# Streaming encoder step: head loads moved from the POOL queue to the SP queue as 64-row pieces, head 0 loaded during the last projection group, one store for both parts of q or k

## The chip, the cores and the metric

The kernel runs on one core of one Trainium2 chip. The metric is device time in microseconds, the median of several executions. TensorE (PE) does the matmuls, VectorE (DVE), ScalarE (ACT) and GpSimd (POOL) the elementwise work; transfers are issued from SyncE's queue (SP) and from POOL's queue.

## What is computed

One layer of a chunk-causal encoder, in float32, over 2048 prompt frames and 8 x 16 sample frames. The part around the change is the mixer:

```python
proj = h @ w_in
q, k, v, u_val, u_gate = jnp.split(proj, [D_ATT, 2 * D_ATT, 3 * D_ATT, 3 * D_ATT + D_CONV], axis=-1)
...
s = jnp.einsum("bqhd,bkhd->bhqk", qc, kc) * scale + bias      # 9-chunk band, 8 heads of 64
p = jax.nn.softmax(s, axis=-1)
att = jnp.einsum("bhqk,bkhd->bqhd", p, vc)
...
u = u_val * jax.nn.sigmoid(u_gate)
c = silu(layernorm(depthwise_conv(u, width 31)))
y = jnp.concatenate([att, c], axis=-1) @ w_out
```

Cross-attention into 256 memory tokens and a SwiGLU feed-forward layer of 2816 hidden channels follow, each with norms and a residual.

## The kernel before, in words

Float32 products are made from two float32r parts, a high part (the rounded value) and a low part (the rest), in three matmuls (`mm3`, L281 to L283). Tokens are tiles of 128: 16 prompt tiles and one sample tile.

`phase_proj` goes through the tiles in three groups of two sub-groups: tiles 0 to 5, 6 to 11, and 12 to 15 with the sample tile. Each group makes the GLU projections (4 blocks), v (L657 stores it), and q and k in four blocks j of 128 channels, two heads each. `qk` evicts one block: ACT writes the high part, DVE the low part, into tiles `qh` and `ql` of two buffers each (in the last group `qhx`, `qlx`), and two stores (L713, L714) put them into the DRAM buffers `qs[j]` and `ks[j]`, laid out [part, channel, token]. The convolution taps run as background generators: `conv_vector` on DVE (L522), `conv_pool` on ACT and POOL (L531, L532), then `conv_norm` (L537 to L557), which transposes on PE, normalizes, goes through tanh and stores.

Normalized inputs of a sub-group lie in the pairs `hh0`/`hl0` to `hh2`/`hl2` in turn, 12 KB a partition each, in the arena `sbR`. The arenas are laid out by hand: a tag is a ring of buffers at an offset in KB, and a later stage's tile on the same bytes waits until the earlier readers are done.

`attention` goes through 8 heads of 16 tiles: `scores` (L845, two matmuls per key range: q's two parts stacked on 128 rows as `q2`, against k's high part on both halves of the rows, `k2`, and the same for the low part, `kl`), `softmax_band` (L760 on DVE with the head's bias tile `bt`, L762 on ACT), `transp` (L862 to L864) four units later, `values` (L875) two units after that, once for four tiles. One sample's attention (`sample`) is interleaved with each head. `load_head` loads a head: q2, k2, kl and v2 on POOL's queue, 1 MB each, and `bt` on SP's queue (L829). Buffers exist for an even and an odd head, so that head h + 2 reuses those of head h. In program order the load of the next head stands at tile 6 of a head.

```python
nc.gpsimd.dma_start(q2[:, :], self.qs[jj][:, rr, :])
for c, dst in ((0, k2), (1, kl)):
    nc.gpsimd.dma_start(dst[:, :], self.ks[jj][c, rr, :].unsqueeze(0).to_broadcast([2, DH, NPT * P]))
nc.gpsimd.dma_start(v2[:, :, :], self.vs[h // 4][:, h % 4, :, :])
```

The order of the instructions on each engine and queue is set by a scheduler that plays the program through with its own costs: it takes what is ready by then, the earlier in the program first (the conv background with a lowered priority). Each engine and queue then runs in that order and waits where it must. `mixout` follows with the output projection; its weights are loaded and split by `out_weights` during the last head.

Of the kernel before, what the change touches and what calls it, by code (L numbers as in the profile page):

```python
# [8 lines left out]
F32 = mybir.dt.float32  # L9
F32R = mybir.dt.float32r  # L10
# [7 lines left out]
P = 128  # L18
D = 1024
KC = D // P  # L20
NPT = 16
S_TILE = 16
H = 8
DH = 64
# [9 lines left out]
NEG = -1e30  # L34
# [102 lines left out]
class Build:  # L137
# [22 lines left out]
    def early(self, ctx):  # L160
        phases = self.phases
        inner = ctx.enter_context(ExitStack())
        fa, fb = self.fa, self.fb = self.flex(ctx, (8192, F32)), self.flex(inner, (4096, F32))
        sbF, sbR, ps = self.sbF, self.sbR, self.ps
        self.w = Region().lay(sbF, 0, ("wf", 4, 3)).lay(sbR, 72, ("wh", 4, 4), ("wl", 4, 4))
        self.psa = Region().lay(ps, 0, ("mm", 2, 4), ("tr", 4, 2))
        self.ap = (Region()
                   .lay(sbF, 12, ("gbc", 4, 1), ("xt", 4, 2), ("junk", 2, 1), ("ut", 3.1171875, 6))
                   .lay(sbF, 12, ("qhx", 1.5, 2), ("qlx", 1.5, 2), ("kxx", 0.5, 2), ("vo", 1, 3), ("ko", 2, 5))
                .lay(sbF, 44.75, ("us", 5.75, 1), ("cwt", 0.484375, 1), ("cvec", 0.0625, 1), ("half", 0.0625, 1))  # L170
                   .lay(fb, 0, ("ct", 3, 5), ("bst", 0.03125, 2), ("bmv", 0.03125, 2), ("ss", 0.03125, 6),
                        ("rstd", 0.03125, 6))
                   .lay(fa, 0, ("xn", 2, 2), ("z", 2, 2), ("th", 2, 1), ("sg", 1.5, 2), 
                        ("ctmp", 3, 2), ("qh", 1.5, 2), ("ql", 1.5, 2), ("kx", 0.5, 2))
                   .lay(sbR, 0, *[(f"h{c}{i}", 12, 1) for i in range(3) for c in "hl"])
                   .lay(sbR, 104, ("vv", 2, 2)))
        smp = Region().lay(fa, 28, ("qsamp", 2, 1), ("ksamp", 2, 1))
        self.qsamp = self.t(smp, [P, 4, P], F32, "qsamp")
        self.ksamp = self.t(smp, [P, 4, P], F32, "ksamp")
        if "mem" in phases:  # L180
            self.phase_mem()
        if "proj" in phases:
            self.phase_proj()
        if "att" not in phases:
            return
        self.kept = Region().lay(sbF, 0, ("attT", 32, 1), ("sums", 0.5, 1), ("attS", 2, 1))
        self.attT = self.t(self.kept, [P, 4, NPT * P], F32, "attT")
        self.sums = self.t(self.kept, [P, NPT, H], F32, "sums")
        self.attS = self.t(self.kept, [P, 4, P], F32, "attS")
        self.attention()  # L190
        inner.close()
        with ExitStack() as c:
            self.mixout(c)
# [251 lines left out]
    def phase_proj(self):  # L445
        nc, A = self.nc, self.A
        pool = self.ap
        ps_mm = ps_tr = Region().lay(self.ps, 0, ("mm", 2, 4), ("tr", 2, 2), ("ca", 4, 1))
        self.lo_engine = nc.gpsimd
        big = [P, KC, 3 * P]  # L450
# [23 lines left out]
        def norm_sub(sub):  # L474
            hh = self.t(pool, big, F32R, f"hh{self.nsub % 3}", 1)
            hl = self.t(pool, big, F32R, f"hl{self.nsub % 3}", 1)
# [99 lines left out]
        for gi, subs in enumerate(GROUPS):  # L576
# [4 lines left out]
            t0 = tiles[0]  # L581
            hs = nxt
            uts = []
# [93 lines left out]
            def qk(which, j, blk, x):  # L677
# [5 lines left out]
                sh = self.t(pool, [P, 3 * P], F32R, "qh" + x_, 2)  # L683
                sl = self.t(pool, [P, 3 * P], F32R, "ql" + x_, 2)
# [56 lines left out]

    def attention(self):
        nc, A = self.nc, self.A
        sbF, sbR, ps, fa, fb = self.sbF, self.sbR, self.ps, self.fa, self.fb
        pool = (Region().lay(sbF, 34.5, ("kc", 4, 2), ("kt", 4.25, 1), ("pp", 1.5, 1), ("vn", 2, 1))
                .at("z", 2.5, (fa, [15, 17.5, 20, 22.5, 25]), (fb, [0, 2.5, 5]))
                .lay(fb, 7.5, ("vc", 4, 2), ("nmx", 0.03125, 12), ("sm", 0.03125, 2))
                .lay(fa, 0, ("qbd", 2.5, 2), ("otmp", 2, 1), ("bs", 1.0625, 1)).lay(fa, 10, ("bt", 2.5, 2))
                .at("q20", 8, (sbR, [0])).at("k20", 8, (sbR, [8])).at("kl0", 8, (sbR, [16])).at("v20", 8, (sbR, [72]))
                .at("q21", 8, (sbR, [24])).at("k21", 8, (sbR, [32])).at("kl1", 8, (sbR, [40])).at("v21", 8, (sbR, [80]))  # L750
                .lay(sbR, 48, ("ph0", 10, 1), ("pl0", 10, 1)).lay(sbR, 88, ("ph1", 10, 1), ("pl1", 10, 1)))
# [3 lines left out]
        row = [P, NPT * P]  # L755
# [61 lines left out]
        def load_head(h):  # L817
            jj, odd = h // 2, h % 2
            rr = slice(odd * DH, (odd + 1) * DH)
            q2 = self.t(pool, row, F32R, f"q2{odd}", 1)  # L820
            k2 = self.t(pool, row, F32R, f"k2{odd}", 1)
            kl = self.t(pool, row, F32R, f"kl{odd}", 1)
            v2 = self.t(pool, [P, NPT, P], F32R, f"v2{odd}", 1)
            nc.gpsimd.dma_start(q2[:, :], self.qs[jj][:, rr, :])
            for c, dst in ((0, k2), (1, kl)):
                nc.gpsimd.dma_start(dst[:, :], self.ks[jj][c, rr, :].unsqueeze(0).to_broadcast([2, DH, NPT * P]))
            nc.gpsimd.dma_start(v2[:, :, :], self.vs[h // 4][:, h % 4, :, :])
            bt = self.t(pool, [P, W5], F32, "bt", 2)
            nc.sync.dma_start(bt[:, :], toep[h][:, :])  # L829
            nc.gpsimd.memset(bt[:DH, W5 - DH:], NEG)  # L830
            nc.gpsimd.memset(bt[DH:, :DH], NEG)
            return q2, k2, kl, v2, bt

# [51 lines left out]
        heads = {0: load_head(0)}  # L885
# [14 lines left out]
        for i in range(n + LV + 1):  # L900
            if i < n:
# [3 lines left out]
                if t == 6 and h + 1 < H:  # L905
                    heads[h + 1] = load_head(h + 1)
# [19 lines left out]
    def selectors(self):  # L926
# [3 lines left out]
            self.sbR, 68, ("expand", 2, 1), ("rt", 0.5, 3), ("rs", 0.0625, 2))  # L930
# [22 lines left out]
    def out_weights(self):  # L953
# [3 lines left out]
        for k, (o, engine) in enumerate(zip((0, 8, 16, 72, 24, 32, 48, 56), "PPPPVPVP")):  # L957
# [9 lines left out]
    def mixout(self, ctx):  # L967
# [10 lines left out]
                .at("kvh", 4, (sbR, [64, 80]), (fr, [8])).at("kvl", 4, (sbR, [104, 84]), (fr, [12])))  # L978
# [706 lines left out]
```

## Time and profile before

| | |
|---|---|
| median of 3 runs | 3066.88 us (3065.92 to 3074.45) |
| span of the profiled execution | 3068.5 us (the page gives no other time of it) |
| PE, DVE, ACT, POOL busy | 96%, 70%, 44%, 46% |
| granted TensorE clock, mean | 0.980 |
| moved by SP's queue, by POOL's queue | 427.53 MB, 69.70 MB |

How to read it: times in a row are microseconds from the start of the span. A row of the timeline is start, duration, engine, line, operation, output <- input, and in brackets how long the engine had stood before it and what ended that. Tiles show as the arena they lie in (sbr, sbx, sbf, flexb, psb for PSUM), DRAM buffers by name. Busy shares are averages over stages; what a stage could give is read from the waits inside it. "Granted clock" is the share of full speed that the throttle gave TensorE.

### The profile page before, as it was taken

How to read it: one execution, taken by the hardware profiler on the slowest of the kernel's cores; microseconds unless marked ns; L12 is line 12 of the kernel's file. 1: busy time of each engine (PE TensorE's matmuls, PEld its weight loads, DVE VectorE, ACT ScalarE, POOL GpSimd, SP SyncE). 2: the span in 40 equal slices, each digit the busy share in tenths (PEclk: the TensorE clock that was granted, in tenths of full speed). 3: DMA queues.
4: the chain of work that ended last, by engine and by line, in shares of the span. 5: the costliest groups of instructions: out<-in, count | busy, mean ns of one | idle time of the engine just before them, and what ended most of it. 6: DMA issues, size and time to landing. Idle time of an engine off the chain costs nothing.

```text
span 3068.5 us, 46049 instructions
## 1 busy us (share of the span) xinstructions
PE 2958.1 (96%) x16924; PEld 2725.9 (89%) x16924; DVE 2135.7 (70%) x3077; ACT 1358.3 (44%) x2718; POOL 1419.9 (46%) x1336
## 2 busy tenths in 40 slices
PE   8999999968999999999999999999999999999998
PEld 8999999957888788788888999999999999888786
DVE  6696886746668456635456888877878999556565
ACT  4544455546767344423234333443334444433432
POOL 0267595621112324325355655555555776524413
PEclk9999999978999999999999999999999999999999
DMA  8635252645663456423246333454425345756664
GB/s 302 246 111 176 90 172 97 189 150 135 155 158 141 147 205 209 168 69 124 91 157 206 132 135 135 149 176 159 154 105 174 144 144 178 261 186 210 217 202 161
DMA packets 217693, 500.17 MB, mean 163 GB/s; under 512 B 40757, under 2 KB 104765, under 8 KB 208627
## 3 DMA queue, kind: packets, MB, share of 16 engines
q1 hardware_dynamic: 181035, 427.53, 41.6%
q0 software_dynamic: 36432, 69.70, 7.3%
q8 instruction: 133, 2.18, 0.3%
q14 instruction: 93, 0.76, 0.1%
HBM read 365.97 MB, written 141.81 MB: 165 GB/s over the span
## 4 chain that ended last, share of the span: by engine, by line
PE 38%; DMA 4%; DVE 3%; issue 2%; POOL 2%; ACT 1%; SPq 0%; DVEq 0%; POOLq 0%; ACTq 0%
PE psb L283 12%; PE psb L282 12%; PE psb L281 12%; DMA sbf<-in_w_down_dram 2%; PE psb L289 1%; POOL sbf L1536 1%; DMA sbf<-x 1%; PE psb L1391 1%; DMA sbf<-hn 0%; DVE sbr L1597 0%; DVE sbr L1540 0%; DVE sbr L1414 0%; POOL sbf L338 0%; DMA sbf<-in_w_gate_dram 0%; DVE flexb L1476 0%
## 5 line engine op out<-in xcount | busy, mean ns | idle before, releaser
L281 PE MATMUL psb<-sbr 128*128 128x384 f32 (+3 forms) x2808 | 945.6, 338 | 11.1 <-DVE sbf L688 7.1
L282 PE MATMUL psb<-sbr 128*128 128x384 f32 (+3 forms) x2356 | 808.5, 343 | 2.6 <-DVE sbr L318 2.4
L283 PE MATMUL psb<-sbr 128*128 128x512 f32 (+3 forms) x1848 | 633.4, 344 | 2.7 <-DVE sbr L1597 2.5
L281 PEld LDWEIGHTS psb<-sbr 128*128 128x128 f32 x2808 | 533.0, 190 | 41.0 <-DVE sbf L688 7.3
L283 PE MATMUL psb<-sbr,sbx 128*128 128x384 f32 (+2 forms) x1484 | 478.5, 323 | 0.0
L282 PEld LDWEIGHTS psb<-sbr 128*128 128x128 f32 x2356 | 448.1, 190 | 29.3 <-DVE sbr L318 2.7
L283 PEld LDWEIGHTS psb<-sbr 128*128 128x128 f32 x1848 | 348.6, 189 | 31.6 <-DVE sbr L1597 4.9
L289 PE MATMUL psb<-sbr 128*128 128x512 f32 x1200 | 295.5, 394 | 3.0 <-DVE flexb L1044 1.7
L1414 DVE TENSOR_TENSOR sbr<-sbf,sbr 128x512 fp32r<-128x512 f32 x258 | 263.5, 1024 | 40.7 <-ACT sbr L1413 40.0
L1413 ACT CAST sbr<-sbf 128x512 fp32r<-128x512 f32 x258 | 159.3, 620 | 280.5 <-PE psb L282 232.3
L283 PEld LDWEIGHTS psb<-sbr,sbx 128*128 128x128 f32 x1484 | 282.7, 191 | 0.1
L522 DVE SCALAR_TENSOR_TENSOR psb<-sbf,psb 128x768 f32<-128x768 f32 (+1 forms) x290 | 264.5, 912 | 6.2
L289 PEld LDWEIGHTS psb<-sbr 128*128 128x128 f32 x1200 | 222.4, 189 | 48.7 <-DVE flexb L1044 2.1
L1597 DVE TENSOR_TENSOR sbr<-sbf,sbr 128x384 fp32r<-128x384 f32 (+1 forms) x231 | 168.4, 752 | 93.7 <-ACT sbr L1596 91.2
L276 POOL TENSOR_TENSOR sbx<-sbf,sbr 128x1024 fp32r<-128x1024 f32 x60 | 150.9, 2517 | 85.8 <-ACT sbr L275 81.2
L1596 ACT CAST sbr<-sbf 128x384 fp32r<-128x384 f32 (+1 forms) x231 | 110.7, 497 | 167.7 <-PE psb L282 150.1
L1536 POOL TENSOR_TENSOR sbf<-sbf 128x512 f32<-128x512 f32 x77 | 105.7, 1377 | 168.3 <-DMA sbf<-in_w_down_dram 166.7
L532 POOL TENSOR_TENSOR flexb<-flexb,flexb 128x128 f32<-128x128 f32 (+1 forms) x180 | 168.5, 936 | 30.9 <-ACT flexb L531 20.3
L281 PE MATMUL psb<-sbr,sbx 128*128 128x384 f32 (+1 forms) x524 | 170.6, 327 | 1.2 <-ACT sbr L1393 0.7
L1413 ACT CAST sbx<-sbf 128x512 fp32r<-128x512 f32 x153 | 94.7, 621 | 161.6 <-PE psb L282 152.7
L1414 DVE TENSOR_TENSOR sbx<-sbf,sbx 128x512 fp32r<-128x512 f32 x153 | 151.5, 992 | 15.7 <-ACT sbx L1413 15.5
L1408 POOL TENSOR_TENSOR sbf<-sbf 128x512 f32<-128x512 f32 x66 | 98.6, 1493 | 107.6 <-DVE sbr L1414 50.8
(339 smaller groups left out, 6294.0 us busy)
## 6 DMA issues: line engine op xcount, KB each, us to landing
af<-flexb SPq DMA_DIRECT2D x33, 1344.0 KB, 5.6
sbf<-in_w_down_dram SPq DMA_DIRECT2D x154, 256.0 KB, 3.9
sbf<-af SPq DMA_DIRECT2D x90, 384.0 KB, 4.0
sbf<-in_w_gate_dram SPq DMA_DIRECT2D x66, 512.0 KB, 3.3
sbf<-in_w_up_dram SPq DMA_DIRECT2D x66, 512.0 KB, 3.5
sbf<-x SPq DMA_DIRECT2D x49, 512.0 KB, 3.9
sbf<-in_w_in_dram SPq DMA_DIRECT2D x48, 512.0 KB, 4.2
sbr<-ks POOLq DMA_DIRECT2D x16, 1024.0 KB, 33.9
```

The costliest lines, as they stand in the source:

```text
L276: self.lo_engine.tensor_tensor(lo[:, :], wf[:, :], hi[:, :].bitcast(F32), ALU.subtract)
L281: nc.tensor.matmul(ps, lh, rh, start=start, stop=False, **kw)
L282: nc.tensor.matmul(ps, lh, rl, start=False, stop=False, **kw)
L283: nc.tensor.matmul(ps, ll, rh, start=False, stop=stop, **kw)
L289: nc.tensor.matmul(y[o], l, r[:, o * 512:(o + 1) * 512], start=start and x == 0, stop=stop and x == 2)
L522: nc.vector.scalar_tensor_tensor(acc if w < CW - 1 else o, src(w), cwt[:, j, w:w + 1], acc, ALU.mult, ALU.add)
L532: nc.gpsimd.tensor_tensor(o, o, v, ALU.add)
L1413: nc.scalar.copy(hs[j][:, :], src[j])
L1414: nc.vector.tensor_tensor(ls[j][:, :], src[j], hs[j][:, :].bitcast(F32), ALU.subtract)
L1536: nc.gpsimd.tensor_tensor(acc[:, :], acc[:, :], q[:, :], ALU.add if s > 0 else ALU.subtract)
L1596: nc.scalar.copy(ch[:, m], a[:, x, m])
L1597: nc.vector.tensor_tensor(cl[:, m], a[:, x, m], ch[:, m].bitcast(F32), ALU.subtract)
```

## The change

- A head is loaded from SP's queue, in seven transfers: k2, q2 and kl each as two pieces of 64 rows (lower half, upper half), and v2. The pieces can cover a range of tiles.
- Head 0 is loaded in two steps: tiles 0 to 11 at the start of the last projection group, tiles 12 to 15 after block j = 0 of q and k in that group. Heads 1 to 7 are loaded whole, at the same place of the program as before.
- Buffers move so that head 0's are free in the last group: the last sub-group (one prompt tile and the sample tile) gets its own smaller pair `hhz`/`hlz` at 56 to 72 KB of `sbR`; `v20`, `ph`/`pl` (the transposed probabilities) and `v21` lie elsewhere; the softmax tiles `z`, the bias tiles `bt`, two of the split output weights and a few small tiles too.
- `qh` and `ql` become one tile `qk` of two parts, and one store writes both.

```diff
-                   .lay(sbF, 12, ("qhx", 1.5, 2), ("qlx", 1.5, 2), ("kxx", 0.5, 2), ("vo", 1, 3), ("ko", 2, 5))
+                   .lay(sbF, 12, ("qkx", 3, 2), ("kxx", 0.5, 2), ("vo", 1, 3), ("ko", 2, 5))
...
+                   .lay(sbR, 56, ("hhz", 8, 1), ("hlz", 8, 1))
...
             hs = nxt
+            if last:
+                first = self.head_tiles(0)
+                self.head_load(0, first, 0, t0)
...
-                nc.sync.dma_start(dst[0, :, col:col + npc], sh[:, :npc].bitcast(F32))
-                nc.sync.dma_start(dst[1, :, col:col + npc], sl[:, :npc].bitcast(F32))
+                nc.sync.dma_start(dst[:, :, col:col + npc].rearrange("c p n -> p c n"),
+                                  sp[:, :, :npc].bitcast(F32))
...
+                if last and j == 0:
+                    self.head_load(0, first, t0, NPT)
+                    self.head0 = first
...
+    def att_pools(self):
+        sbF, sbR, fa, fb = self.sbF, self.sbR, self.fa, self.fb
+        self.attp = (Region().lay(sbF, 34.5, ("kc", 4, 2), ("kt", 4.25, 1), ("pp", 1.5, 1), ("vn", 2, 1))
+                     .at("z", 2.5, (fa, [24]), (fb, [0, 2.5, 5]), (fa, [9, 11.5, 14, 16.5]))
+                     .lay(fb, 7.5, ("vc", 4, 2), ("nmx", 0.03125, 12), ("sm", 0.03125, 2))
+                     .lay(fa, 0, ("qbd", 2.5, 2), ("otmp", 2, 1), ("bs", 1.0625, 1)).lay(fa, 19, ("bt", 2.5, 2))
+                     .lay(sbR, 0, ("q20", 8, 1), ("k20", 8, 1), ("kl0", 8, 1), ("q21", 8, 1), ("k21", 8, 1), ("kl1", 8, 1),
+                          ("v20", 8, 1), ("ph1", 10, 1), ("pl1", 10, 1), ("v21", 8, 1))
+                     .lay(sbR, 88, ("ph0", 10, 1), ("pl0", 10, 1)))
+
+    def head_tiles(self, h):
+        nc, pool, odd = self.nc, self.attp, h % 2
+        row = [P, NPT * P]
+        q2, k2, kl = [self.t(pool, row, F32R, f"{n}{odd}", 1) for n in ("q2", "k2", "kl")]
+        v2 = self.t(pool, [P, NPT, P], F32R, f"v2{odd}", 1)
+        bt = self.t(pool, [P, 5 * P], F32, "bt", 2)
+        nc.sync.dma_start(bt[:, :], self.toep[h][:, :])
+        nc.gpsimd.memset(bt[:DH, 5 * P - DH:], NEG)
+        nc.gpsimd.memset(bt[DH:, :DH], NEG)
+        return q2, k2, kl, v2, bt
+
+    def head_load(self, h, tiles, a, b):
+        nc = self.nc
+        q2, k2, kl, v2, _ = tiles
+        c = slice(a * P, b * P)
+        rr = slice(h % 2 * DH, (h % 2 + 1) * DH)
+        for o in range(2):
+            half = slice(o * DH, (o + 1) * DH)
+            for dst, src in ((k2, self.ks[h // 2][0]), (q2, self.qs[h // 2][o]), (kl, self.ks[h // 2][1])):
+                nc.sync.dma_start(dst[half, c].bitcast(F32), src[rr, c])
+        nc.sync.dma_start(v2[:, a:b, :].bitcast(F32), self.vs[h // 4][:, h % 4, a:b, :])
...
-                .at("z", 2.5, (fa, [15, 17.5, 20, 22.5, 25]), (fb, [0, 2.5, 5]))
...
-        heads = {0: load_head(0)}
+        heads = {0: self.head0}
...
-                    heads[h + 1] = load_head(h + 1)
+                    heads[h + 1] = self.head_tiles(h + 1)
+                    self.head_load(h + 1, heads[h + 1], 0, NPT)
...
-        for k, (o, engine) in enumerate(zip((0, 8, 16, 72, 24, 32, 48, 56), "PPPPVPVP")):
+        for k, (o, engine) in enumerate(zip((0, 8, 16, 48, 24, 32, 72, 56), "PPPPVPVP")):
```

More of the change, by code (lines that the diff above doesn't have):

```diff
@@ L173, in early @@
                    .lay(fa, 0, ("xn", 2, 2), ("z", 2, 2), ("th", 2, 1), ("sg", 1.5, 2),
-                        ("ctmp", 3, 2), ("qh", 1.5, 2), ("ql", 1.5, 2), ("kx", 0.5, 2))
+                        ("ctmp", 3, 2), ("qk", 3, 2), ("kx", 0.5, 2))
                    .lay(sbR, 0, *[(f"h{c}{i}", 12, 1) for i in range(3) for c in "hl"])
+                   .lay(sbR, 56, ("hhz", 8, 1), ("hlz", 8, 1))
                    .lay(sbR, 104, ("vv", 2, 2)))
@@ L179, in early @@
         self.ksamp = self.t(smp, [P, 4, P], F32, "ksamp")
+        self.att_pools()
         if "mem" in phases:
@@ L449, in phase_proj @@
         self.lo_engine = nc.gpsimd
-        big = [P, KC, 3 * P]
         gbc = self.gain(pool, "g_mix_pre", "gbc")
@@ L474, in norm_sub @@
         def norm_sub(sub):
-            hh = self.t(pool, big, F32R, f"hh{self.nsub % 3}", 1)
-            hl = self.t(pool, big, F32R, f"hl{self.nsub % 3}", 1)
+            x = self.nsub % 3 if len(sub) == 3 else "z"
+            hh, hl = [self.t(pool, [P, KC, len(sub) * P], F32R, f"h{c}{x}", 1) for c in "hl"]
             self.nsub += 1
@@ L682, in qk @@
                 tick()
-                sh = self.t(pool, [P, 3 * P], F32R, "qh" + x_, 2)
-                sl = self.t(pool, [P, 3 * P], F32R, "ql" + x_, 2)
+                sp = self.t(pool, [P, 2, 3 * P], F32R, "qk" + x_, 2)
+                sh, sl = sp[:, 0, :], sp[:, 1, :]
                 col = t0 * P + (hs[0][3] if x else 0)
@@ L742, in attention @@
     def attention(self):
         nc, A = self.nc, self.A
-        sbF, sbR, ps, fa, fb = self.sbF, self.sbR, self.ps, self.fa, self.fb
-        pool = (Region().lay(sbF, 34.5, ("kc", 4, 2), ("kt", 4.25, 1), ("pp", 1.5, 1), ("vn", 2, 1))
-                .at("z", 2.5, (fa, [15, 17.5, 20, 22.5, 25]), (fb, [0, 2.5, 5]))
[L747 to L751, printed above, removed]
+        ps, pool = self.ps, self.attp
@@ L754, in attention @@
         toep = self.toep
-        row = [P, NPT * P]
         def softmax_band(ps, w, bias, sm):
@@ L815, in sample @@
             nc.vector.tensor_copy(self.attS[DH:, :, ss], po[DH:, :, DEC_S:])
[L817 to L832, printed above, removed]
         def scores(hd, t, sm):
@@ L929, in selectors @@
         pool = self.wp = Region().lay(self.fa, 27.5, ("eye", 0.03125, 1), ("rc", 0.03125, 2)).lay(
-            self.sbR, 68, ("expand", 2, 1), ("rt", 0.5, 3), ("rs", 0.0625, 2))
+            self.sbR, 84, ("expand", 2, 1), ("rt", 0.5, 3), ("rs", 0.0625, 2))
         eye = self.t(pool, [2 * H, H], F32, "eye")
@@ L977, in mixout @@
                 .lay(sbR, 96, ("sTh", 4, 1), ("sTl", 4, 1))
-                .at("kvh", 4, (sbR, [64, 80]), (fr, [8])).at("kvl", 4, (sbR, [104, 84]), (fr, [12])))
+                .at("kvh", 4, (sbR, [64, 80]), (fr, [8])).at("kvl", 4, (sbR, [68, 104]), (fr, [12])))
         ps_y = ps_p = ps_so = Region().lay(self.ps, 0, ("y", 2, 3), ("p", 2, 3), ("so", 4, 1))
```

## The prediction

> **What bounds the kernel now.** I read the page first, then the table of windows, the waits of PE, the list of DMA issues, and last the timeline of single engines around the places those had named.
>
> ```profile
> span 3068.5 us, 46049 instructions
> PE 2958.1 (96%) x16924; PEld 2725.9 (89%) x16924; DVE 2135.7 (70%) x3077; ACT 1358.3 (44%) x2718; POOL 1419.9 (46%) x1336
> ...
> PE   8999999968999999999999999999999999999998
> ...
> PEclk9999999978999999999999999999999999999999
> ```
>
> The profiled execution's span is 1.6 us above the median of the runs (3066.88); the page gives no other time for it, and I subtract gains from the median. PE is busy 96% of the span, so only a stage where PE stands still has anything to give. The one visible hole is in slice 9 of 40 (614 to 690 us), where the granted clock also falls. The windows show how far that stage reaches:
>
> ```profile
> 600.00:700.00 100.00, 65.96 (x361) 58.56 (x360) 50.14 (x101) 46.15 (x131) 25.71 (x51) 0.79 0.47 144
> 700.00:800.00 100.00, 94.69 (x604) 88.94 (x603) 68.56 (x167) 69.68 (x164) 12.88 (x23) 0.89 0.64 144
> 800.00:900.00 100.00, 86.42 (x575) 81.01 (x573) 66.98 (x161) 67.73 (x160) 13.19 (x22) 0.90 0.71 155
> 900.00:1000.00 100.00, 99.66 (x615) 89.02 (x615) 77.61 (x161) 71.61 (x152) 24.80 (x19) 0.97 0.42 145
> ```
>
> Columns are PE, PEld, DVE, ACT, POOL busy, the clock, the DMA share, GB/s. From 600 to 900 us (end of the projection, then attention) PE loses some 53 us to idling and runs at a granted clock of 0.79 to 0.90. At 900 to 1000 it is full: attention without waits is bound by PE. The first row of PE's waits from 655 to 1000 us (total, times, longest) says for whom:
>
> ```profile
> PE psb L845 <- DMA sbr<-qs: 16.7, 3, 6.6
> ```
>
> Scores (L845) wait three times for a head's q load. The list of DMA issues says why (KB of one, microseconds to landing):
>
> ```profile
> sbf<-in_w_gate_dram SPq DMA_DIRECT2D x66, 512.0 KB, 3.3
> ...
> sbr<-ks POOLq DMA_DIRECT2D x16, 1024.0 KB, 33.9
> ...
> sbr<-qs POOLq DMA_DIRECT2D x8, 1024.0 KB, 34.8
> ...
> qs<-flexb SPq DMA_DIRECT2D x32, 192.0 KB, 2.2
> ...
> f2s<-flexb SPq DMA_DIRECT2D x4, 1024.0 KB, 7.4
> ...
> qs<-sbf SPq DMA_DIRECT2D x8, 192.0 KB, 12.4
> ```
>
> A megabyte on POOL's queue takes 34 us, on SP's 7.4. And the same q store that lands in 2.2 us in the first two groups (from flexb) takes 12.4 in the last one (from sbf), beside the first head loads. While three such loads are alone (791 to 796 us) the queue moves little and uses few engines:
>
> ```profile
> q0 software_dynamic: 71, 0.58, 30.1%
> ```
>
> 0.58 MB in 5 us is 116 GB/s at a time worth 4.8 of the 16 DMA engines, so three loads (3.15 MB) need 27 us at least; any 16-engine store that meets them waits for the busy few.
>
> The Trainium skill, page "DMA: Bandwidth & Descriptors", section "Rules for kernel authors", has the reason: a DMA whose outermost dimension is c below 16, a leading broadcast of copies above all, is confined to c engines. The loads L824 and L826 lead with a dimension of 2, so by it three of them use 6 engines, which the 4.8 above agrees with, and the 64-row pieces would use all 16.
>
> **Part 1, loads of heads 1 to 7 (POOL to SP, 64-row pieces).** POOL loses four issues a head and SP gains seven. The v loads on POOL mark the ends of heads 0 to 5:
>
> ```profile
> 726.55 0.58 POOL L827 DMA_DIRECT2D sbr<-vs  x1 [7.77 <-PE psb L875]
> 767.16 0.57 POOL L827 DMA_DIRECT2D sbr<-vs  x1 [6.26 <-PE psb L875]
> 799.92 0.57 POOL L827 DMA_DIRECT2D sbr<-vs  x1 [9.85 <-PE psb L875]
> 841.30 0.57 POOL L827 DMA_DIRECT2D sbr<-vs  x1 [8.44 <-PE psb L875]
> 871.92 0.57 POOL L827 DMA_DIRECT2D sbr<-vs  x1 [5.21 <-PE psb L875]
> 916.00 0.57 POOL L827 DMA_DIRECT2D sbr<-vs  x1 [7.45 <-PE psb L875]
> ```
>
> The distances are 40.6, 32.8, 41.4, 30.6 and 44.1 us, mean 37.9. Two parities of buffers alternate: a head's load may start when the head two before it has made its scores, so it has one head's time to land, and 34 us is too long for every other head. The unhindered heads take (32.8 + 30.6)/2 = 31.7; the other three lose 8.9 + 9.7 + 12.4 = 31.0 us. That is the upper bound of the gain; the lower is 16.7, the PE waits for qs alone, with nothing for the clock that falls after them. I take 28, near the upper end, because the clock rows (0.89, 0.90) say that the loss goes on after the wait, and 3 less since the two unhindered heads are not all heads.
>
> It stands only if the new load fits into 31.7 us. A head is 4.19 MB. At the rate of the first 100 us, where SP's queue loads at its hardest,
>
> ```profile
> 0.00:100.00 100.00, 86.75 (x657) 84.06 (x658) 67.77 (x109) 49.16 (x90) 6.34 (x20) 1.00 0.80 279
> ```
>
> it is 15.0 us; as eight single 512 KB transfers of 3.3 us one after another, 26.4. Both fit. What is late next is PE itself.
>
> Against the pieces stands another rule of the Trainium skill's same section: transfers to disjoint partition halves are no use, they serialize, and one of 128 partitions is better. By it the pieces would win nothing from being two, and the load would lie nearer to 26.4 than to 15; the trace of before has no 64-row load to set against it. It is the ground of the slower rival below.
>
> SP's added issues: seven at the 0.34 us of a bias load (its row stands with the rivals) are 2.4 us a head, and SP mostly waits in this stage. POOL's freed 3 us a head gain nothing: POOL is under 14% busy there.
>
> **Part 2, head 0 by pieces during the last group.** Twelve of sixteen token tiles (3.15 MB) go out when group 2 starts, the rest (1.05 MB) after the j = 0 q and k. Group 2 starts near 475 us:
>
> ```profile
> 400.00:500.00 100.00, 100.00 (x626) 99.82 (x626) 66.42 (x87) 54.91 (x98) 80.04 (x68) 1.00 0.45 148
> ...
> 622.00:630.00 8.00, 7.84 (x48) 7.64 (x46) 6.15 (x11) 3.25 (x10) 4.35 (x10) 0.69 0.71 219
> ```
>
> PE stands nowhere from 400 to 500 us and the DMA engines have half their time free, so a burst of 11 us (3.15 MB at 279 GB/s) costs nothing; the cover is the weight blocks loaded ahead (three in float, four split), and if they ran out PE would lose what the burst exceeds them by. In the last group the following stalls have the old loads behind them (PE rows, each with the rows of the engine it waited for):
>
> ```profile
> 593.96 0.82 POOL L824 DMA_DIRECT2D sbr<-qs  x1 [5.51 <-DMA qs<-sbf]
> 595.31 0.41 ACT L531 ACTIVATE flexb<-sbf 128x128 f32<-128x128 f32 x1 [4.55 <-POOL flexb L532]
> 596.26 0.48 PE L703 MATMUL psb<-ident,sbf 128*128 128x128 f32 x1 [4.24 <-ACT sbf L701]
> ...
> 616.82 0.29 DVE L694 TENSOR_TENSOR sbf<-psb,sbf 128x128 fp32r<-128x128 f32 x1 [3.26 <-DMA qs<-sbf]
> 621.46 0.58 PE L281 MATMUL psb<-sbr 128*128 128x256 f32 x1 [7.11 <-DVE sbf L688]
> ...
> 668.10 0.28 ACT L687 ACTIVATE sbf<-psb 128x128 fp32r<-128x128 f32 x1 [8.60 <-DMA qs<-sbf]
> 669.13 1.11 PE L862 MATMUL psb<-ident,flexb 128*128 128x128 f32 x4 [8.17 <-ACT flexb L762]
> ...
> 677.18 0.50 PE L845 MATMUL psb<-sbr 128*128 128x256 f32 x2 [2.34 <-DVE flexb L760]
> ...
> 697.46 0.44 DVE L760 CUSTOM_DVE_ANT_0 flexb<-psb,flexb 128x272 f32<-128x272 f32 x1 [6.45 <-DMA flexb<-toep]
> 697.97 1.01 PE L845 MATMUL psb<-sbr 128*128 128x384 f32 x2 [6.05 <-DVE flexb L760]
> ```
>
> - 4.2 us: POOL sits in front of head 0's q load until a q store has landed; ACT's scaled copies, queued behind POOL's adds, hold the copy that PE's transposes need. The wait moves to SP, where only a store's landing (2.2 us) is behind it. Gone: 4.2 (bounds 0 to 4.2).
> - 7.1 us: DVE's and ACT's evictions wait for the two-deep store buffers, whose stores share engines with the q load. Gone: 7.1 (0 to 7.1). The 48 matmuls after it take 8.0 us at a clock of 0.69 (the 622 to 630 row), where 0.69 of it would do at full clock, so 2 more go.
> - 8.2 and 2.3 us: the last q store behind head 1's 4 MB. These loads still start when the last projection frees their buffers, now in the same queue as the store. I take half, 5.2 (bounds −4, a burst of 15 us wholly ahead of the store in place of 11, to 10.5).
> - 6.0 us: the sample's bias rows, behind the k output stores and head 1's loads. Gone: 6.0 (0 to 6.0).
>
> Sum 24.5. About 8 us of idle around 630 to 645 us, conv norms that PE waits on, I leave.
>
> **Part 3, one store for q's or k's two parts.** 48 SP issues of 0.32 us fewer (one per q or k block and sub-group) on a queue that mostly waits: 0. The buffer is freed when both halves have landed, which it needed before as well: 0, bounds ±1, since the high part's store now waits for DVE's 0.5 us.
>
> **Part 4, moved buffers.** Softmax tiles 2 to 4 now lie on the conv tiles and tile 5 on the tanh buffer, all held until the sample tile's conv norm is through; before, the first five did not. That chain takes about 9 us and runs beside the first four units: I charge 3 (bounds 0 to 16, had it ended where it does now). The last two weight blocks of the output projection now lie on buffers that the last values matmuls read, so their split comes after these; their matmuls are the last of the first tile: 2 (0 to 5).
>
> **Sum:** 28 + 24.5 − 3 − 2 = 47.5. 3066.88 − 47.5 = 3019.
>
> **The rivals.**
> - *The transition keeps its stalls.* SP issues head 1's burst ahead of the last stores, and the softmax buffers wait for the conv norm, so Part 2 and 4 come to nothing: 28 us, 3039. For it: two 4 MB movers meet at 655 us in either kernel. Against: head 0 is out of the way.
> - *SP's queue holds the loads: slower.* SP itself waits, in order, for other things in this stage:
>
> ```profile
> SPq L829 <- DVE flexb L760: 75.3, 6, 16.8
> SPq L769 <- PE psb L812: 55.7, 5, 16.5
> ...
> 736.85 0.86 POOL L826 DMA_DIRECT2D sbr<-ks  x1 [3.30 <-PE psb L845]
> ...
> 739.29 0.34 SPq L829 DMA_DIRECT2D flexb<-toep  x1
> ```
>
> If a head's pieces stand behind such a wait of 16.5 us and take 26.4, they need 42.9 us, 5.0 more than the mean head today: six heads lose 30, the transition gives 19.5, and the time is 3077. It turns slower where delay plus load passes 37.9 + 19.5/6 = 41.2 us. Against it: POOL's loads start within 3 us of SP's bias load for the same head (the last two rows), so the queues are in step. A delay plus load of 38 to 41 us would be the case of no change: the loads move and take as long.
> - *The conv chain loosens too.* DVE's waits for stores from 590 to 624 us go, its conv taps end earlier, the 8 us around 637 and the 5.2 kept above shrink: another 20, 2999.
>
> **How the numbers follow.** Forecast 0.62, transition kept 0.18, conv chain too 0.11, no change 0.04, slower 0.05. Faster by over 0.3% (9 us, about what this kernel's measurement can tell from nothing) is 0.91, same 0.04, slower 0.05. The range, 2992 to 3051, holds the first three with the bounds of Part 1 (11 less) and Part 4.
>
> **What would show it.** Right: head loads on SP's queue landing under 20 us, no PE wait for qs, v loads an even 31 to 33 us apart, q stores from sbf near 3 us, clock above 0.95 from 700 to 900. Wrong: heads still 38 apart, or SP's pieces with landings near 30; or a PE hole of over 8 us at the start of attention before softmax tiles, which is the first rival.

## The result, and the profile after

The changed kernel takes 3033.39 us (median of 4 runs, 3033.04 to 3034.92) against 3070.66 us for the kernel before (its three runs and one more beside the changed one): a ratio of 0.9872, 95% interval 0.9854 to 0.9890. It is faster by 37 us. In a second set of runs the same file took 3035.93 us, ratio 0.9876 (0.9861 to 0.9892). The profiled execution is one of 3033.59 us; its span is 36.7 us shorter than that of before. From the page of the changed kernel:

```profile
span 3031.8 us, 45992 instructions
...
PE 2949.8 (97%) x16924; PEld 2715.4 (90%) x16924; DVE 2138.1 (71%) x3077; ACT 1357.7 (45%) x2718; POOL 1397.0 (46%) x1304
...
PE   8999999979999999999999999999999999999998
...
PEclk9999999989999999999999999999999999999999
```

PE does the same 16924 matmuls. The hole in slice 9 is one tenth shallower, slice 10 has filled, and the granted clock of both is a tenth higher. The table of windows, in the same columns as before:

```profile
600.00:700.00 100.00, 79.62 (x475) 71.38 (x474) 60.20 (x131) 56.74 (x156) 17.70 (x39) 0.85 0.53 143
700.00:800.00 100.00, 100.00 (x675) 94.13 (x675) 78.31 (x188) 79.15 (x185) 4.50 (x12) 0.95 0.73 178
800.00:900.00 100.00, 99.28 (x660) 93.12 (x659) 78.00 (x188) 79.29 (x180) 11.32 (x13) 0.93 0.57 151
900.00:1000.00 100.00, 92.50 (x474) 76.72 (x474) 59.14 (x100) 48.72 (x99) 27.45 (x27) 0.97 0.44 148
```

PE idles 20.4 us from 600 to 700 (34.0 before), and from 700 to 900 only 0.7 us (18.9 before): attention is now bound by PE. But two things stand here that were not forecast. The clock from 700 to 900 is 0.95 and 0.93, not full, although PE stands nowhere. And 900 to 1000, the window that was full before, now has 7.5 us of idle. It does not hold the same work: the output projection, which began after 969 us, now begins after 923.

The list of DMA issues (KB of one, median microseconds to landing):

```profile
sbr<-ks SPq DMA_DIRECT2D x28, 512.0 KB, 10.2
...
sbr<-vs SPq DMA_DIRECT2D x7, 1024.0 KB, 4.9
sbr<-qs SPq DMA_DIRECT2D x14, 512.0 KB, 10.7
...
PE psb L812 <- ACT sbf L813: 5.1, 1, 5.1
```

A piece lands in 10 us where the megabyte took 34. The last row is now the first of PE's waits from 655 to 1000 us, and no row of that list names a load of q or k. The v loads, now on SP's queue, mark the ends of heads 0 to 5 as before:

```profile
699.24 0.34 SPq L781 DMA_DIRECT2D sbr<-vs  x1
735.14 0.34 SPq L781 DMA_DIRECT2D sbr<-vs  x1
769.55 0.32 SPq L781 DMA_DIRECT2D sbr<-vs  x1
800.80 0.33 SPq L781 DMA_DIRECT2D sbr<-vs  x1
835.29 0.33 SPq L781 DMA_DIRECT2D sbr<-vs  x1
868.46 0.32 SPq L781 DMA_DIRECT2D sbr<-vs  x1
```

The distances are 35.9, 34.4, 31.3, 34.5 and 33.2, mean 33.8: more even than before, but in the mean 2 us above the 31.7 of an unhindered head. Against the rows of before (726.55 and 916.00) the changed kernel is 27.3 us ahead at the end of head 0 and 47.5 at the end of head 5. Where the lead goes after that is read from the last scores (PE) and the eighth store of x after the output projection (POOL, with two rows of before for comparison):

```profile
969.00 0.79 PE L845 MATMUL psb<-sbr 128*128 128x384 f32 x4
...
1105.68 0.62 POOL L1046 DMA_DIRECT2D x<-flexb  x1 [0.30 <-POOL flexb L1045]
```

```profile
922.68 0.79 PE L861 MATMUL psb<-sbr 128*128 128x384 f32 x4
...
1067.58 0.63 POOL L1063 DMA_DIRECT2D x<-flexb  x1 [0.30 <-POOL flexb L1062]
```

The lead is 46.3 us at the last scores and 38.1 us at the eighth store: the output projection gives 8.2 us back (136.7 us from mark to mark before, 144.9 after). What follows it keeps the rest, within 2 us. At the place of the loss the timeline shows ACT late with the split of a weight block (L277), and PE standing 5 of 25 us:

```profile
945.30 1.05 ACT L277 CAST sbr<-sbf 128x1024 fp32r<-128x1024 f32 x1 [5.56 <-PE psb L891]
...
951.66 4.14 PE L291 MATMUL psb<-sbr 128*128 128x512 f32 x10 [0.86 <-DVE sbr L278]
...
940.00:965.00 25.00, 19.93 (x81) 15.06 (x80) 12.65 (x19) 9.44 (x17) 6.37 (x6) 0.86 0.49 156
```

ACT waits 5.56 us for L891, the values matmuls: the block's buffer is one that they read. The last row is the window's.

### The profile page after: what moved, and what is told of

Read it like the earlier page. It is cut to its first block, busy times and chain, and to the rows that moved or that the text cites. A ratio compares the mean times of both kernels' runs of the same rounds, so it can differ in the third digit from the quotient of the medians.

```text
span 3031.8 us, 45992 instructions
## 1 busy us (share of the span) xinstructions
PE 2949.8 (97%) x16924; PEld 2715.4 (90%) x16924; DVE 2138.1 (71%) x3077; ACT 1357.7 (45%) x2718; POOL 1397.0 (46%) x1304
## 4 chain that ended last, share of the span: by engine, by line
PE 40%; DMA 3%; DVE 3%; POOL 2%; issue 1%; ACT 1%; SPq 0%; DVEq 0%; POOLq 0%; ACTq 0%
PE psb L285 13%; PE psb L284 13%; PE psb L283 13%; DMA sbf<-in_w_down_dram 1%; PE psb L291 1%; DMA sbf<-x 1%; POOL sbf L1553 1%; DVE sbr L1614 1%; PE psb L1408 1%; DMA sbf<-hn 0%; DVE sbr L1431 0%; POOL sbf L340 0%; DMA hn<-sbf 0%; DVE flexb L1493 0%; DMA sbf<-in_w_gate_dram 0%
## 5 line engine op out<-in xcount | busy, mean ns | idle before, releaser
L283 PEld LDWEIGHTS psb<-sbr 128*128 128x128 f32 x2808 | 531.2, 189 | 34.4 <-ACT sbr L1613 2.8
L1553 POOL TENSOR_TENSOR sbf<-sbf 128x512 f32<-128x512 f32 x77 | 108.0, 1407 | 167.9 <-DMA sbf<-in_w_down_dram 166.1
L533 POOL TENSOR_TENSOR flexb<-flexb,flexb 128x128 f32<-128x128 f32 (+1 forms) x180 | 169.4, 941 | 22.3 <-ACT flexb L532 12.8
L277 ACT CAST sbr<-sbf 128x1024 fp32r<-128x1024 f32 x98 | 102.7, 1051 | 107.2 <-PE psb L284 57.6
```

The lines of the kernel that those rows point to most:

```text
L283: nc.tensor.matmul(ps, lh, rh, start=start, stop=False, **kw)
L533: nc.gpsimd.tensor_tensor(o, o, v, ALU.add)
L1553: nc.gpsimd.tensor_tensor(acc[:, :], acc[:, :], q[:, :], ALU.add if s > 0 else ALU.subtract)
```

## The experiments

Each time stands beside runs of the kernel before on the same chip, and a ratio is to those. Their median is 3071.28 us for the first run of 1 and for 2 and 3; 3073.87 for 4, 5, 6 and the first kernel of 7; 3072.70 for the repeat in 1, the second kernel of 7 and 8. Between the chips and batches, compare ratios; inside a profile, marks: "end of head 0" and "end of head 5" are the v loads above, "last scores" and "eighth store" the other two. The changed kernel's marks in a second profile (from the second set of runs, an execution of 3029.77 us) were 698.48, 866.24, 921.71 and 1063.36, so they repeat within 2.3 us up to the last scores and 4.2 us at the eighth store.

**1. Part 1 alone, on the kernel before** (all heads, head 0 too, loaded at the old place):

```diff
-            nc.gpsimd.dma_start(q2[:, :], self.qs[jj][:, rr, :])
-            for c, dst in ((0, k2), (1, kl)):
-                nc.gpsimd.dma_start(dst[:, :], self.ks[jj][c, rr, :].unsqueeze(0).to_broadcast([2, DH, NPT * P]))
-            nc.gpsimd.dma_start(v2[:, :, :], self.vs[h // 4][:, h % 4, :, :])
+            for o in range(2):
+                half = slice(o * DH, (o + 1) * DH)
+                for dst, src in ((k2, self.ks[jj][0]), (q2, self.qs[jj][o]), (kl, self.ks[jj][1])):
+                    nc.sync.dma_start(dst[half, :].bitcast(F32), src[rr, :])
+            nc.sync.dma_start(v2[:, :, :].bitcast(F32), self.vs[h // 4][:, h % 4, :, :])
```

> The kernel before with Part 1 alone: all eight heads, head 0 included, loaded at the old places of the program from SP's queue, k2, q2 and kl as 64-row pieces; buffers and the two stores as before. Theory (the two-row leading dimension kept a load on few DMA engines, and the pieces use all of them): each piece lands in about 10 us as in the changed kernel, PE's waits for qs go, heads 33 to 34 us apart, and the part of the transition gain that came from loads hogging a few engines comes too: 3040, within 8. If the transition gain came from loading head 0 early, only the heads' 19 us come: 3048 to 3052. Rival (the queue order on SP holds loads and stores up): 3060 or more.

Measured: 3027.58 us, ratio 0.9859 (0.9832 to 0.9886), against 0.9872 for the whole change. Part 1 was expected to give only a part of the gain; it gives all of it and more. The experiment was run again beside the changed kernel on one chip:

> Part 1 alone once more, on the same chip as the changed kernel. Theory (Parts 2 to 4 together lose: the last weight blocks cost more than head 0 early wins): 4 to 8 us faster than the changed kernel of this call. Rival (the difference of 6 us between the two lay in the chips and calls): within 2 us of it.

> The changed kernel, nothing changed, beside the next three on one chip: how far its stage marks move from one profiled execution to another. If the marks (end of head 0 at 699, last scores at 923, eighth x1 store at 1068) return within 1 us, the differences of 3 to 8 us between kernels in these stages are the kernels'; if they move by 3 us or more, only the difference between with and without pieces is shown.

Measured: 3026.55 us, 0.9848 (0.9835 to 0.9862), against 3035.93 us, 0.9876 (0.9861 to 0.9892). Part 1 alone is 9 us below the whole change; the two intervals just touch, and so do the times (at most 3029.61 against at least 3029.77). Its marks (the repeat's rows: ends of heads 0 and 5, last scores):

```profile
710.55 0.33 SPq L828 DMA_DIRECT2D sbr<-vs  x1
...
870.37 0.32 SPq L828 DMA_DIRECT2D sbr<-vs  x1
...
921.03 0.83 PE L846 MATMUL psb<-sbr 128*128 128x384 f32 x4
```

With Part 1 alone the end of head 0 already comes 16.0 us earlier than before; the changed kernel is another 11.3 us ahead of that. By the end of head 5 the 11.3 have shrunk to 1.9, and at the last scores the changed kernel is 1.7 us behind. Its heads take 33.8 us, those of Part 1 alone 32.0. Neither has more than 2 us of PE waits from 699 to 921. What differs is the granted clock. Windows of the changed kernel, then of Part 1 alone (second column PE busy, last but two the clock):

```profile
700.00:740.00 40.00, 40.00 (x272) 37.53 (x272) 31.87 (x77) 32.33 (x75) 1.74 (x5) 0.96 0.79 205
740.00:780.00 40.00, 40.00 (x263) 37.53 (x262) 30.53 (x73) 30.49 (x71) 1.77 (x5) 0.91 0.58 142
780.00:820.00 40.00, 40.00 (x289) 38.15 (x287) 32.62 (x80) 33.42 (x80) 2.19 (x5) 0.99 0.74 177
820.00:860.00 40.00, 40.00 (x255) 37.28 (x255) 30.18 (x72) 29.74 (x68) 1.49 (x4) 0.88 0.69 164
```

```profile
700.00:740.00 40.00, 40.00 (x281) 37.89 (x280) 32.95 (x79) 32.39 (x76) 1.79 (x6) 0.99 0.76 187
740.00:780.00 40.00, 40.00 (x284) 38.09 (x283) 32.13 (x79) 33.55 (x79) 2.69 (x6) 1.00 0.69 181
780.00:820.00 40.00, 39.87 (x290) 37.66 (x289) 33.07 (x79) 33.68 (x77) 1.49 (x4) 1.00 0.64 156
820.00:860.00 40.00, 40.00 (x268) 37.84 (x267) 30.69 (x77) 30.07 (x74) 1.49 (x4) 0.93 0.77 182
```

PE is busy all but 0.2 us in both, and the rows count 1079 matmuls in one against 1123 in the other. The mean clock is 0.935 against 0.980: 0.045 of 160 us is 7.2 us, most of the 9.4 lost over five heads. These two profiles are the far ends, though. In the other profile of each kernel the clock over the same 160 us is 0.95 against 0.97, and the heads take 33.6 and 32.6 us. The kernels of 4 to 8 that are built on the changed one have 0.94 to 0.97, Part 1 with one store (7) has 0.98, and the pieces on POOL's queue (2), with the old buffers and head 0 at the old place, 0.94. So the low clock does not need the early head 0 or the moved buffers; what sets it no run isolates.

**2. Is it the pattern or the queue?** Two kernels on the kernel before: the 64-row pieces on POOL's queue (the loop of 1 with `nc.gpsimd`), and the old wide loads on SP's queue (the old four lines with `nc.sync`).

> The kernel before with the 64-row pieces, but still issued from POOL's queue. Theory (it is the access pattern): pieces land in 10 to 16 us, no PE wait for qs, time within 8 us of the kernel with pieces on SP's queue. Rival (POOL's queue is slow by itself): pieces land in 25 us or more, PE waits for qs of over 10 us in all, time 3060 to 3070 as before.

> The kernel before with its old 1 MB loads (leading dimension 2) unchanged in pattern, but issued from SP's queue. Theory (the pattern confines each load to two engines, and by what the changed kernel showed nothing else is wrong): loads land no faster than before, 25 us at best, and if all three of a head sit on the same two engines 60 us or more; then the heads are 60 us apart and the time is above 3150; with the engines taken in turn as on POOL it is 3060 to 3075. Rival (POOL's queue was the cause): loads land in 5 to 12 us and the time is near that of the kernel with pieces on SP's queue.

Pieces on POOL: 3038.07 us, 0.9893 (0.9871 to 0.9915). Most of the gain without moving a queue. From its DMA list and its windows (a head's load in flight; the third row is POOL's queue in that window):

```profile
sbr<-ks POOLq DMA_DIRECT2D x32, 512.0 KB, 10.2
...
692.00:704.00 12.00, 12.00 (x64) 11.08 (x63) 6.05 (x15) 6.08 (x16) 0.29 (x2) 0.72 1.14 220
...
q0 software_dynamic: 342, 2.20, 94.9%
```

POOL's queue alone moves 2.20 MB in 12 us, 183 GB/s at the time of 15 engines, where three wide loads moved 116 GB/s on 4.8; with SP's queue it is 220 GB/s at a DMA share of 1.14. The changed kernel shows the same on SP's queue, 234 GB/s at a share of 1.01:

```profile
687.00:699.00 12.00, 12.00 (x79) 11.43 (x78) 9.04 (x22) 8.94 (x22) 0.29 (x2) 0.90 1.01 234
```

What the queue adds is some 10 us (3038.07 against 3027.58; the times do not overlap, the intervals of the ratios do).

Wide loads on SP: 3355.68 us, 1.0927 (1.0903 to 1.0952). Heads are 70.4 us apart. A window inside it, the queue's share in the same window, three waits from 655 to 1255 us (PE for a head's load, POOL for the bias, PE for POOL) and one issue on SP's queue:

```profile
840.00:890.00 50.00, 38.02 (x246) 35.96 (x246) 27.06 (x64) 27.70 (x64) 1.47 (x4) 0.84 0.14 53
...
q1 hardware_dynamic: 443, 2.64, 13.6%
...
PE psb L845 <- DMA sbr<-ks: 44.0, 2, 22.2
...
POOL flexb L830 <- DMA flexb<-toep: 420.2, 7, 70.0
...
PE psb L802 <- POOL flexb L797: 112.2, 5, 38.6
...
851.12 17.78 SPq L826 DMA_DIRECT2D sbr<-ks  x1
```

13.6% of 16 engines is 2.2 engines, and 53 GB/s is less than half of what the same loads got on POOL's queue: with several of them in flight, little more than two engines are at work. Single issues on SP's queue last 17.78 us here and up to 20.5 elsewhere in attention. The longest waits are for what stands behind the loads in that queue: POOL waits 420.2 us for the heads' bias tiles, and PE 112.2 for the sample's rows that POOL scales (L797) only after that. The Trainium skill, page "DMA: Bandwidth & Descriptors", section "Why a DMA increments its semaphore by 16 and not by 1", says that a transfer confined to k engines takes the lowest-numbered k when SP issues it, and k engines in turn when POOL does. The 2.2 and the 4.8 engines agree with it. Pattern and queue are not two small terms that add: without the pieces the move to SP costs 9%, with them it gains some 10 us.

**3. Parts 2 to 4 alone** (the changed kernel, heads 1 to 7 loaded by POOL's four wide transfers again):

```diff
-                    self.head_load(h + 1, heads[h + 1], 0, NPT)
+                    q2, k2, kl, v2, _ = heads[h + 1]
+                    jj, rr = (h + 1) // 2, slice((h + 1) % 2 * DH, ((h + 1) % 2 + 1) * DH)
+                    nc.gpsimd.dma_start(q2[:, :], self.qs[jj][:, rr, :])
+                    for c, dst in ((0, k2), (1, kl)):
+                        nc.gpsimd.dma_start(dst[:, :],
+                                            self.ks[jj][c, rr, :].unsqueeze(0).to_broadcast([2, DH, NPT * P]))
+                    nc.gpsimd.dma_start(v2[:, :, :], self.vs[(h + 1) // 4][:, (h + 1) % 4, :, :])
```

> The changed kernel with heads 1 to 7 loaded as before (POOL's queue, 1 MB loads with a leading dimension of 2); head 0 early by pieces, the buffers moved, one store: Parts 2 to 4 alone. Theory: the heads are 37 to 38 us apart again, which gives back the 19 us that the changed kernel won between the heads, and the last q store waits again beside head 1's load (another 5 to 8): 3055 to 3062. Rival (the early head 0 sets the pace of the later heads): heads stay at 34, 3035 to 3042.

Measured: 3084.87 us (3066.21 to 3098.65), ratio 1.0038 (1.0012 to 1.0063). A miss: no gain, but a loss of 0.4%, with times 32 us apart. From its DMA list and PE's waits in attention:

```profile
sbr<-ks POOLq DMA_DIRECT2D x14, 1024.0 KB, 35.4
...
PE psb L861 <- DMA sbr<-qs: 18.6, 2, 17.2
```

Its end of head 0 is 714.63, 11.9 us ahead of before, and its heads are 37.7 us apart, as the theory had it; the lead at the end of head 5 is 12.8 us. At the last scores (964.08) 4.9 are left, and the output projection then takes 146.2 us to the eighth store (136.7 before), so that the kernel is 4.6 us behind there. The profile is one of 3074.50 us; what makes the median another 10 us longer stands in no profile.

**4. Head 0 early or late** (the changed kernel with head 0 loaded whole, in pieces, at the start of attention):

```diff
-            if last:
-                first = self.head_tiles(0)
-                self.head_load(0, first, 0, t0)
...
-        heads = {0: self.head0}
+        heads = {0: self.head_tiles(0)}
+        self.head_load(0, heads[0], 0, NPT)
```

> The changed kernel with head 0 loaded whole where attention begins in the program, its buffers free as early as in the changed kernel. Theory (what the transition won came from the pieces, no longer on few engines, with some 10 us from the early head 0, as the ends of head 0 in the changed kernel, 699, and with Part 1 alone, 710, say): 5 to 11 us slower than the changed kernel, 3039 to 3045. Rival (the scheduler places the loads by when they are ready, so the place in the program says little): within 3 us of the changed kernel.

Measured: 3035.66 us, 0.9874 (0.9855 to 0.9893), the ratio of the changed kernel. The end of head 0 comes at 706.80, 7.6 us later than in the changed kernel, and the last scores at 926.61, 3.9 later; the total shows nothing of it beyond its noise.

**5. The last weight blocks** (the changed kernel, blocks 6 and 7 on buffers that the last values matmuls do not read, and the small tiles that lay there moved):

```diff
-        for k, (o, engine) in enumerate(zip((0, 8, 16, 48, 24, 32, 72, 56), "PPPPVPVP")):
+        for k, (o, engine) in enumerate(zip((0, 8, 16, 48, 24, 32, 88, 96), "PPPPVPVP")):
...
-                .at("mh", 4, (sbR, [40, 88])).at("ml", 4, (sbR, [44, 92]))
-                .lay(sbR, 96, ("sTh", 4, 1), ("sTl", 4, 1))
-                .at("kvh", 4, (sbR, [64, 80]), (fr, [8])).at("kvl", 4, (sbR, [68, 104]), (fr, [12])))
+                .at("mh", 4, (sbR, [40, 56])).at("ml", 4, (sbR, [44, 60]))
+                .lay(sbR, 64, ("sTh", 4, 1), ("sTl", 4, 1))
+                .at("kvh", 4, (sbR, [72, 80]), (fr, [8])).at("kvl", 4, (sbR, [76, 104]), (fr, [12])))
```

> The changed kernel with the last two blocks of the output weights (woh6, wol6, woh7, wol7) at 88 to 104 KB, on ph0 and pl0, whose last readers are the values of the third quad of the last head, not of the fourth; the first tile's second buffers, the sample's tiles and the memory tiles take 56 to 84 KB instead. Theory (the moved weight blocks hold up the first tile of the output projection): from the last scores to the eighth x1 store it takes 137 to 139 us as before in place of 144.9, and the time is 6 to 8 us below the changed kernel, 3026. Rival (the loss there comes from another order of the queues): no more than 2 us below, 3031 to 3035.

Measured: 3030.03 us, 0.9860 (0.9839 to 0.9882). Its window over the start of the output projection, and its marks:

```profile
930.00:960.00 30.00, 30.00 (x148) 24.43 (x147) 20.03 (x29) 13.80 (x26) 9.97 (x10) 1.00 0.60 193
...
919.53 0.82 PE L861 MATMUL psb<-sbr 128*128 128x384 f32 x4
...
1054.09 0.63 POOL L1063 DMA_DIRECT2D x<-flexb  x1 [0.30 <-POOL flexb L1062]
```

PE stands nowhere and the clock is full; last scores to eighth store is 134.6 us, 10.3 shorter than in the first profile of the changed kernel and 7.1 shorter than in its second. All six profiles with the late blocks need 141.6 to 146.2 us there, all eight others 134.6 to 138.5. So this place costs what the output projection gives back. In the total only some 4 to 5 us of it show, inside the intervals: the stage after, cross-attention, is longer here. From the eighth store to the last store of its normalized rows (L1338) it takes 599.5 us in this profile and 590.7 in the changed kernel's, and why is open.

**6. The order of the softmax buffers** (the changed kernel, the ones on the tanh and conv tiles used in another order):

```diff
-                     .at("z", 2.5, (fa, [24]), (fb, [0, 2.5, 5]), (fa, [9, 11.5, 14, 16.5]))
+                     .at("z", 2.5, (fa, [24, 11.5, 14, 16.5]), (fb, [0, 2.5, 5]), (fa, [9]))
```

> The changed kernel with the softmax tiles 2 to 4 on the GLU and conv scratch at 11.5 to 19 KB, free earlier, and those on the conv tiles later in the ring. Theory (my charge of 3 us for tiles that wait for the sample tile's conv norm): the end of head 0 comes 2 to 4 us earlier, 3030. Rival (that chain is through before the softmax needs the tiles, as no wait of PE or DVE on it shows in the changed kernel): within 1.5 us of the changed kernel, 3032 to 3035.

Measured: 3032.38 us, 0.9863 (0.9838 to 0.9887); end of head 0 699.78 against 699.24 and 698.48. No wait for the conv tiles shows.

**7. One store or two.** The changed kernel with two stores again, and Part 1 alone with one store added:

```diff
-                nc.sync.dma_start(dst[:, :, col:col + npc].rearrange("c p n -> p c n"),
-                                  sp[:, :, :npc].bitcast(F32))
+                nc.sync.dma_start(dst[0, :, col:col + npc], sh[:, :npc].bitcast(F32))
+                nc.sync.dma_start(dst[1, :, col:col + npc], sl[:, :npc].bitcast(F32))
```

> The changed kernel with two stores for the two parts of q or k again. Theory (Part 3 is worth nothing, SP has time): within 2 us of the changed kernel, 3031 to 3036. Rival (48 issues more on SP, which now has the loads as well, make the stores late where the evictions wait for them, in the last group): 4 us or more slower.

> Part 1 alone with one store for the two parts of q or k. Theory (one store is worth nothing, within 2 us of Part 1 with two stores). Rival (one store costs, as 3026.8 with two against 3033.4 with one in the changed kernel would have it: the larger store lands later and frees its buffer later): 4 to 7 us slower than Part 1 with two stores.

With two stores the changed kernel took 3026.77 us, 0.9849 (0.9825 to 0.9873). That looked like a cost of the one store. Where it can be seen by itself, it shows none: Part 1 with one store took 3025.82 us, 0.9846 (0.9833 to 0.9860), Part 1 with two on the same chip 3026.55. The first interval overlaps that of the changed kernel, so no effect of the stores is shown.

**8. The changed kernel with the weight blocks of 5 and the two stores of 7:**

> The changed kernel with both the last weight blocks at 88 to 104 KB and two stores: the version meant to beat both. Theory (the weight blocks' place costs 7 to 8 us in the output projection, two stores cost nothing): eighth x1 store near 1054, time 3022 to 3027, below the changed kernel of this call by 6 to 10. Rival (what the output projection wins, the stage after it gives back, as in the kernel with the weight blocks alone, 3030): within 4 us of the changed kernel.

Measured: 3024.80 us (3021.49 to 3031.06), 0.9849 (0.9835 to 0.9862). It is below the kernel before by 48 us and below the changed kernel on the same chip by 11, with intervals that just meet; it is level with Part 1 alone. Early loading and moved buffers, repaired, still win nothing over the pieces that these runs can tell.

## Why the prediction was right, and where it was not

The time forecast was 3019 us, the median came out at 3033.39; the ratio times the median that the forecast started from gives 3027.6, so about 8 us of the 47.5 did not come. That the sum came so near is in part luck, for its terms were shared out wrongly. The pieces alone, head 0's at the old place among them, won 44 to 46 us (experiment 1), where 28 were forecast for those of heads 1 to 7. The early load, the moved buffers and the one store add nothing to that and may cost up to 9 us, and without the pieces of heads 1 to 7 they win nothing (3), where 19.5 of gain were forecast for Parts 2 to 4. The two errors offset each other. By its steps:

- **The bound** held. Head loads that use few engines were what heads waited for. With the pattern changed, on either queue, the waits for q are gone (experiments 1 and 2); with only the rest changed they stay (3). The rule of the Trainium skill that stands in the prediction, a leading dimension of 2 confines a transfer to few engines, agrees with these runs. The rule against transfers to halves of the rows, which stands there too, did not decide: a piece lands in 10 us in a burst of seven, on either queue, at 220 to 234 GB/s. No run loads q or k in a single transfer with 128 rows leading, as that rule prefers.
- **Part 1, 28 us.** By itself it gives 29.6 us over five heads in one profile (189.4 to 159.8) and 26.5 in the other, close to the term. In the changed kernel five heads give 20.2, since they take 33.8: the step that failed is that a head without a wait takes 31.7 us. The two unhindered heads from which that was read ran at a clock of 0.95 and 1.00; the changed kernel had 0.935 in these heads. A head's length times its clock, an estimate, is 31.3 to 31.9 us in the two profiles of each kernel, so the length fits at full clock, and the clock is what was missed. Two of the prediction's own signs did not come either: the v loads are 31.3 to 35.9 us apart, not 31 to 33, and the clock from 700 to 900 is not above 0.95.
- **Part 2, 24.5 us less 3 for the softmax buffers.** The lead at the end of head 0 is 27.3 us where 21.5 were forecast. At the first conv norm it is 14.0, near the 13.3 of the first two stalls; the rest, 13.3 against 8.2, comes behind it. The stalls were the right ones, but the cure was ascribed to the wrong part: pieces at the old place bring 16.0 of the 27.3. There the q stores of the last group land in 3.9 us, 12.4 before, as the DMA list of Part 1 alone shows (first run). With the pieces on POOL's queue they still take 10.9, and ACT still waits 7.98 us for the last of them (the second and third row):

```profile
qs<-sbf SPq DMA_DIRECT2D x8, 192.0 KB, 3.9
...
qs<-sbf SPq DMA_DIRECT2D x8, 192.0 KB, 10.9
...
658.12 0.28 ACT L687 ACTIVATE sbf<-psb 128x128 fp32r<-128x128 f32 x1 [7.98 <-DMA qs<-sbf]
```

Yet head 0 ends at 711.82 there, 14.7 us ahead of before. PE's stall of 7.1 us is gone with the pieces on either queue (0.3 at most is left), as the prediction's mechanism, stores that meet a few busy engines, would have it. For the last q store that mechanism is not borne out. POOL's queue took the time of 10.7 engines around that wait before (66.7% of 16, 658 to 668 us) and takes that of 14.0 with the pieces (87.4%, 648 to 660 us), and the store waits about as long. On SP's queue the pieces at the old place leave 0.8 to 1.4 us of that wait, but the one for the sample's bias rows grows from 6.45 to 10.3 and 11.5 us. Early loading and the new buffers bring 11.3, and these are lost again by the last scores. So Part 2 moved a mark and not the end.

The stalls that are left in the changed kernel's transition, in the rows that answer to those of the prediction:

```profile
620.44 1.97 PE L550 MATMUL psb<-ident,flexb 128*128 128x128 f32 x8 [3.45 <-DVE flexb L546]
...
656.66 0.28 ACT L691 ACTIVATE sbf<-psb 128x128 fp32r<-128x128 f32 x1 [3.34 <-DMA qs<-sbf]
...
671.53 0.44 DVE L793 CUSTOM_DVE_ANT_0 flexb<-psb,flexb 128x272 f32<-128x272 f32 x1 [4.28 <-DMA flexb<-toep]
```

ACT's wait for the last q store fell from 8.60 to 3.34 us, a little more than the half that was taken. The wait for the sample's bias rows was to go whole; 4.28 of 6.45 stayed. The conv-norm hole was left in the sum and stayed, so the rival of the conv chain did not come true; it starts 14 us earlier (616.92 against 630.90 for the first statistics).

- **Part 3, 0.** No run contradicts it (experiment 7).
- **Part 4.** The 3 us for the softmax buffers show nowhere (6). The 2 us for the last weight blocks, bounded at 5, are 7.0 in that stage (the mean of the six profiles with the late blocks, 143.44, less that of the eight others, 136.46): the second mis-sized term, outside its bounds. The step took only the split's own delay behind the values matmuls; in the trace ACT stands 5.56 us, PE waits in several places behind it, and the clock falls to 0.86.

The measured time lies between the forecast and the first rival's 3039 us, but that rival's cause, stalls that stay in the transition, is not what happened: the 27.3 us there were won. The slower rival, SP's queue holding the loads, did not occur: issues of one head go out within 4 to 6 us and the v loads are 31 to 36 us apart. With the old pattern something of its kind did occur, and more strongly than it was priced: 3355.68 us.

Open: what sets the granted clock in heads where PE is busy throughout (0.935 to 0.98 among kernels with pieces), why the last q store of the projection waits with the pieces on POOL's queue and not on SP's, and why cross-attention's length moves by 9 us between kernels that differ only ahead of it.

## What to carry to other kernels

Look first at how many DMA engines a slow transfer uses: its share of 16 engines beside its rate told 4.8 engines before anything was changed, and reshaping it so that rows lead was worth 33 us on the old queue and 44 to 46 on the other. Do not credit a fix with stalls that another part of the same change also cures; a mark that moves early counts only if the next stage keeps the lead. When buffers are moved to make room, ask who reads them last at the far end of the stage as well as at the near one.

## What had not been expected of the hardware

- The same wide loads are far worse on SP's queue (2.2 engines, 53 GB/s) than on POOL's (4.8 engines, 116 GB/s), and issues on that queue last up to 20.5 us.
- PE busy without a gap can still run at a granted clock of 0.88 to 0.96 over 40 us (changed kernel, 820 to 860 and 700 to 740), so a stage without waits is not yet a stage at full speed.
